# Output projections: first token differences moved to GpSimd, upper tokens stored aside in four pieces

## The chip, the cores and the metric

The kernel runs on one core of one Trainium2 chip, with that core's engines: TensorE for products (PE in the profile; PEld is its weight load), VectorE (DVE), ScalarE (ACT), GpSimd (POOL) and SyncE (SP), which issues most loads. The metric is the device time of one execution in microseconds; lower is better. A comparison rests on the median of several executions.

## The reference

A two-layer encoder step over 512 prompt frames and 128 sample frames (640 tokens in all), with 2048 channels. What matters here is the end of each layer:

```python
y = jnp.concatenate([y_a, y_b, y_c], axis=-1) @ w_out
return x + y, new_conv, new_k, new_v
```

The concatenation has 2048 channels and `w_out` is 2048 x 2048. After the last layer a final RMSNorm is applied. Everything is fp32, and the outputs must hold that precision.

## The kernel before

Activations lie channel-first: `R` holds 16 blocks of 128 channels by 640 tokens. The 640 tokens are cut into two halves of 320: `TA` (lower) and `TB` (upper). A fp32 product is made of three products of split operands: `split` (L136 to L144) writes a high part on ACT (L138, a copy to the reduced type) and a low part on DVE (L139, raw minus high, so both of its inputs lie in SBUF). `HL` holds both parts of the 16 blocks.

Each layer (the loop at L906) runs 36 projections of `w_in` (`proj`, matmuls at L760) with attention, convolution and gates worked in between. When its last gates are done (L1061 multiplies the last of them into `R`), all 16 blocks of `R` are split into `HL` (L1072, L1073), and the output projection begins.

Output columns 0 and 1 are made by `proj` in the plain way. From column 2 on, columns are taken in pairs by `s_pair` (matmuls in `s_mm`, L821), which saves one of eight products of 768 channels by a Strassen-like scheme: sums and differences of weight tiles and of activation blocks. The activation part is made by `combos` (L794), once a layer, and called after column 1 has been written into the program. With `KA` for blocks 10 to 15 and `KB` for blocks 4 to 9, each in two groups of three blocks (10 to 12 and 13 to 15, with 4 to 6 and 7 to 9), it forms for each group, in place in `R`:

- first, R[KA, TA] becomes R[KA, TB] - R[KA, TA] (L804)
- second, R[KA, TB] becomes R[KB, TB] - R[KA, TB] (L805)
- third, R[KB, TB] becomes R[KB, TB] minus the result of the first (L806)
- fourth, inside the loop that splits the results, R[KB, TA] minus the result of the second (L812)

These are eight subtractions a layer of 128 x 960 fp32, all issued through the helper `sub` on DVE (L789). The results are split into `th`, `tl` and, for the one that has its place there, `HL` (L814).

The second subtraction overwrites the upper tokens of blocks 10 to 15. In the last layer those are needed again for the last two output columns, which are made in another way. So they are stored aside in DRAM first (`y12d`, L1074: one DMA of 960 KB issued by GpSimd after the 16 splits) and loaded back near the end (L1098). The second subtraction waits for that store to have read its source.

Instructions stand in the order of each engine's own queue, and an engine works its queue in order. The order is made by a planner from an estimated timeline, with the loads and splits of weights (`s_prep`, `s_split`, `wprep`) at high priority. SP issues the weight loads (L149). GpSimd's queue carries memsets, small copies and many DMAs: the residual of columns 0 and 1 (L1111, into `zt`), the residual of the pairs (L834) and the store aside. Column 0 and 1 are added to their residual on DVE at L1115.

Of the kernel before, what the change touches and what calls it, by code (L numbers as in the profile page):

```python
# [13 lines left out]
ALU = mybir.AluOpType  # L14
# [4 lines left out]
L = 2  # L19
# [39 lines left out]
def build(nc, tc, ctx, A):  # L59
# [15 lines left out]
    def open_pool(n, side):  # L75
        uid[0] += 1
        held_pools[n] = tc.tile_pool(name=f"{n}{uid[0]}", bufs=1, reuse_waits="tile", side=side)
        cur[n] = held_pools[n].__enter__()

    def close_pool(n):  # L80
        held_pools.pop(n).__exit__(None, None, None)

    def tl(shape, tag, bufs, dt=F32, pl=None):
        uid[0] += 1
        pl = pl or (cur[home[tag]] if tag in home else sb)
        return pl.tile(shape, dt, tag=tag, name=f"{tag}_{uid[0]}", bufs=bufs)

    def w25():
        return tl([P, TOK], "w25", 2)
# [22 lines left out]
    ve, ac, gp, pe, sy = nc.vector, nc.scalar, nc.gpsimd, nc.tensor, nc.sync  # L112

    HL = sb.tile([P, 2 * NK, TOK], F32R, tag="HL", name="HL")
    R = sb.tile([P, NK, TOK], F32, tag="R", name="R")
# [8 lines left out]
    ks = Rf[:, (C0 + 3) * TOK + 288:(C0 + 3) * TOK + 288 + P]  # L124
# [4 lines left out]
    y12d = dr.tile([P, 6, HT], F32, tag="y12d", name="y12d")  # L129
# [3 lines left out]
    def half(t):  # L133
        return t.rearrange("p (s n) -> p s n", s=2)

    def split(raw, scale=None, hi=None, lo=None):  # L136
        if scale is None:
            a = ac.activation(hi, raw, AF.Copy)  # L138
            v = ve.tensor_tensor(out=lo, in0=raw, in1=hi.bitcast(F32), op=ALU.subtract)  # L139
        else:  # L140
            a = ac.activation(hi, raw, AF.Copy, scale=scale)
            v = ve.scalar_tensor_tensor(
                out=lo, in0=raw, scalar=scale, in1=hi.bitcast(F32), op0=ALU.mult, op1=ALU.subtract
            )  # L144
        return a.ins, v.ins
# [99 lines left out]
    def lsm(l, base, n=1):  # L245
        o = l * SM_L + base
        return sm[:, o:o + n]
# [149 lines left out]
    for l in range(L):  # L397
        ve.tensor_scalar(
            out=hsm[:, l * 8:(l + 1) * 8], in0=lsm(l, SM_LG, 8), scalar1=0.5, scalar2=None, op0=ALU.mult
# [366 lines left out]
    KS, KB, KA = slice(0, 4), slice(4, 10), slice(10, 16)  # L766
    TA, TB = slice(0, HT), slice(HT, TOK)
# [20 lines left out]
    def sub(out, a, b):  # L788
        ve.tensor_tensor(out=out, in0=a, in1=b, op=ALU.subtract)  # L789

    def hl(ks, cs):
        return HL[:, ks, cs], HL[:, slice(NK + ks.start, NK + ks.stop), cs]

    def combos():  # L794
        T = {}
        tt = [
            (tl([P, 6, HT], f"th{n}", 1, F32R, cur["tt"]), tl([P, 6, HT], f"tl{n}", 1, F32R, cur["tt"]))
            for n in (2, 3, 4)
        ]
        T[2], T[3], T[4] = tt  # L800
        T[1] = hl(KA, TB)
        gs = [(slice(KA.start + g, KA.start + g + 3), slice(KB.start + g, KB.start + g + 3)) for g in (0, 3)]
        for a, b in gs:
            sub(R[:, a, TA], R[:, a, TB], R[:, a, TA])  # L804
            sub(R[:, a, TB], R[:, b, TB], R[:, a, TB])  # L805
            sub(R[:, b, TB], R[:, b, TB], R[:, a, TA])  # L806
        place = {1: (0, TA), 2: (1, TB), 3: (0, TB), 4: (1, TA)}
        for n in (3, 2, 4, 1):
            for g, ab in enumerate(gs):
                i, cs = place[n]  # L810
                if n == 4:
                    sub(R[:, ab[1], TA], R[:, ab[1], TA], R[:, ab[1], TB])  # L812
                ks = slice(3 * g, 3 * g + 3)
                split(R[:, ab[i], cs], None, T[n][0][:, ks, :], T[n][1][:, ks, :])  # L814
        return T
# [90 lines left out]
    for l in range(L):  # L906
# [35 lines left out]
        for n, (kind, i) in enumerate(ZT):  # L942
# [9 lines left out]
            if l == 0 and 2 <= n < 10:  # L952
                for h in (n - 2, n + 6):
                    a = bscr[h:h + 1, :]
# [13 lines left out]
            elif kind == "ag":  # L968
# [5 lines left out]
                    out=half(u[:, HALO:HALO + 512]), in0=t3[:, :, :PT_], scalar=1.0, in1=a3[:, :, :PT_],  # L974
# [3 lines left out]
                    out=us[:, :, HALO:].rearrange("p (s b) n -> p s b n", s=2),  # L978
                    in0=t3[:, :, PT_:].rearrange("p s (b n) -> p s b n", n=ST), scalar=1.0,
                    in1=a3[:, :, PT_:].rearrange("p s (b n) -> p s b n", n=ST), op0=ALU.add, op1=ALU.mult,  # L980
# [7 lines left out]
            elif kind in ("k", "v"):  # L988
# [4 lines left out]
                if kind == "k":  # L993
                    kk = [[tl([P, 512], t + n, 1, F32R) for n in ("h", "l")] for t in ("k", "m")]
                    for h in range(2):
                        for o in range(2):
                            ac.activation(kk[0][h][rows2[o]], raw[rows2[h]], AF.Copy)
                        for o in range(2):
                            ve.tensor_tensor(
                                out=kk[1][h][rows2[o]], in0=raw[rows2[h]], in1=kk[0][h][rows2[h]].bitcast(F32),  # L1000
                                op=ALU.subtract,
                            )
                    gp.dma_start(A["o_kn"][l], ks)
                else:
# [5 lines left out]
                    for h in range(2):  # L1010
# [3 lines left out]
                            out=V[h][:, :, rows2[1 - h]], in0=pt[:, :, rows2[h]], in1=hi.bitcast(F32),  # L1014
                            op=ALU.subtract,
# [7 lines left out]
            elif kind == "q":  # L1023
# [5 lines left out]
                for h in range(2):  # L1029
# [4 lines left out]
                        out=q[rows2[1 - h]], in0=raw[rows2[h]], in1=hi.bitcast(F32), op=ALU.subtract  # L1034
# [33 lines left out]

        close_pool("at")
        open_pool("sw", "left")  # L1070
        for k in range(NK):
            split(R[:, k, :], None, HL[:, k, :], HL[:, NK + k, :])  # L1072
        if l == L - 1:  # L1073
            gp.dma_start(y12d, R[:, KA, TB])  # L1074
        acc = w25()
        resid = A["xT"] if l == 0 else x1d
        done = NK if l == 0 else NK - 2
# [30 lines left out]
        for j in list(range(2)) + list(range(2, done, 2)):  # L1108
            if j < 2:
                res = zt()  # L1110
                gp.dma_start(res, resid[j])  # L1111
                ps = proj(
                    [A["w_out"][l, j][:, c * 512:(c + 1) * 512] for c in range(4)], s_prep if j else wprep
                )
                ve.tensor_tensor(out=half(R[:, j, :]), in0=ps[:, :, :HT], in1=half(res), op=ALU.add)  # L1115
            else:
                s_pair(l, j, T, resid, turn if j + 2 == done else None)
            if j == 0:
                close_pool("wp")
                open_pool("tt", "right")  # L1120
            if j == 1:
                T = combos()
            for i in range(j, j + 1 if j < 2 else j + 2):
                if l == 0:
                    gp.dma_start(x1d[i], R[:, i, :])
                add_sq(i, i == 0, acc)
# [48 lines left out]
    for i, cs in enumerate(parts):  # L1175
        for k in range(NK):
            with tc.issue_after(last["rsqrt"] if k >= 13 else (evac if k >= 10 else added if k >= 2 else evac0).ins):
                ve.scalar_tensor_tensor(  # L1178
                    out=R[:, k, cs], in0=R[:, k, cs], scalar=sm[:, SM_FG + k:SM_FG + k + 1], in1=rows[i],
# [120 lines left out]
```

## Time and profile before

| | us |
|---|---|
| median of 3 runs | 1834.02 (1833.66 to 1834.88) |
| profiled execution, its own time | 1833.57 |
| its span in the trace | 1831.8 |
| PE busy in the span | 1803.6 (98%) |
| DVE busy | 1258.1 (69%) |
| ACT busy | 785.0 (43%) |
| POOL busy | 174.0 (9%) |

Times in rows are microseconds from the start of the span unless marked ns. A row of the timeline gives start, length, engine, line, operation, what is written and read, the count of merged instructions and, in brackets, how long the engine had been idle before and what released it. Two DVE instructions in a row overlap a little in the records: the next one starts before the recorded end of the one ahead, so the pitch from start to start is what an instruction costs its queue.

### The profile page before, as it was taken

What the parts mean: (1) busy time and instruction counts of PE and PEld (TensorE: products, weight loads), DVE (VectorE), ACT (ScalarE), POOL (GpSimd) and SP (SyncE); (2) the same over time, 40 slices, a digit from 0 to 9 for tenths busy, and PEclk for the clock granted to TensorE, in tenths of its full rate; (3) what the DMA queues carried; (4) which work ended last, traced back from release to release, by engine and by line L of the source; (5) the groups of instructions that cost most, each with busy time, mean ns of one, the idle gap of its engine ahead of it and who ended that gap; (6) DMA issues with size and microseconds to landing.
All of it is one profiled execution on the core that took longest, in us unless ns stands there. A gap on an engine that the chain in (4) does not pass through costs nothing.

```text
span 1831.8 us, 32312 instructions
## 1 busy us (share of the span) xinstructions
PE 1803.6 (98%) x12580; PEld 1766.5 (96%) x12580; DVE 1258.1 (69%) x2562; ACT 785.0 (43%) x1593; POOL 174.0 (9%) x383
## 2 busy tenths in 40 slices
PE   8999999999999999999999999999999999999996
PEld 7899999999999999999999999999999999989996
DVE  7959999567555445966686999766655544776765
ACT  7831224556644334533352222555755333533331
POOL 1121210000001010100030010000001110010000
PEclk9999999999999999999999999999999999999998
DMA  8844442222222343533333332222222244442233
GB/s 283 290 129 103 105 130 76 70 64 70 87 78 84 98 162 116 171 134 116 109 102 89 82 81 78 78 67 73 73 84 85 74 139 132 158 160 84 71 113 121
DMA packets 89193, 202.30 MB, mean 110 GB/s; under 512 B 12064, under 2 KB 17104, under 8 KB 89008
## 3 DMA queue, kind: packets, MB, share of 16 engines
q1 hardware_dynamic: 68848, 139.75, 25.3%
q0 software_dynamic: 17728, 57.60, 10.3%
q10 hardware_dynamic: 2464, 2.88, 0.5%
q8 instruction: 99, 1.62, 0.4%
q14 instruction: 54, 0.44, 0.1%
HBM read 184.84 MB, written 20.33 MB: 112 GB/s over the span
## 4 chain that ended last, share of the span: by engine, by line
PE 94%; DVE 3%; DMA 2%; issue 1%; ACT 0%; SPq 0%; DVEq 0%; ACTq 0%; POOLq 0%
PE z L760 59%; PE a L821 9%; PE z L821 9%; PE a L278 2%; PE z L301 2%; PE a L497 2%; PE a L540 2%; PE a L477 2%; PE z L1145 1%; DVE R L1178 1%; PE a L528 1%; DMA wr<-w_in 1%; PE a L647 1%; PE a L673 1%; PE a L686 1%
## 5 line engine op out<-in xcount | busy, mean ns | idle before, releaser
L760 PE MATMUL z<-HL,wh 128*128 128x320 f32 x4992 | 979.5, 312 | 0.0
L760 PEld LDWEIGHTS z<-HL,wh 128*128 128x128 f32 x4992 | 788.9, 188 | 7.9 <-issue 5.3
L760 PE MATMUL z<-HL,wl 128*128 128x320 f32 x2496 | 580.4, 311 | 0.7 <-DVE wl L139 0.7
L760 PEld LDWEIGHTS z<-HL,wl 128*128 128x128 f32 x2496 | 419.3, 188 | 2.0 <-DVE wl L139 1.0
L138 ACT ACTIVATE wh<-wr 128x512 fp32r<-128x512 f32 x316 | 198.7, 629 | 448.6 <-PE z L760 373.1
L139 DVE TENSOR_TENSOR wl<-wr,wh 128x512 fp32r<-128x512 f32 x316 | 218.0, 690 | 172.7 <-ACT wh L138 163.6
L425 DVE SCALAR_TENSOR_TENSOR R<-R,sm 128x128 f32<-128x128 f32 (+1 forms) x480 | 235.4, 552 | 0.1
L138 ACT ACTIVATE sh<-sr 128x768 fp32r<-128x768 f32 (+1 forms) x125 | 98.3, 787 | 206.2 <-PE a L821 91.4
L821 PE MATMUL z<-HL,sh 128*128 128x320 f32 x728 | 160.9, 309 | 1.9 <-ACT sh L138 1.9
L139 DVE TENSOR_TENSOR sl<-sr,sh 128x768 fp32r<-128x768 f32 (+1 forms) x125 | 110.1, 881 | 40.7 <-ACT sh L138 40.5
L821 PEld LDWEIGHTS z<-HL,sh 128*128 128x128 f32 x728 | 121.7, 188 | 2.4 <-ACT sh L138 2.4
L821 PE MATMUL z<-HL,sl 128*128 128x320 f32 x364 | 113.4, 312 | 0.9 <-DVE sl L139 0.7
L139 DVE TENSOR_TENSOR g<-a,g 128x512 fp32r<-128x512 f32 x80 | 49.5, 634 | 39.8 <-ACT g L138 39.2
L821 PE MATMUL a<-th,sh 128*128 128x320 f32 x234 | 72.2, 308 | 0.0
L821 PE MATMUL a<-tl,sh 128*128 128x320 f32 x234 | 72.2, 308 | 0.0
L821 PE MATMUL a<-th,sl 128*128 128x320 f32 x234 | 72.2, 308 | 0.0
L821 PEld LDWEIGHTS z<-HL,sl 128*128 128x128 f32 x364 | 68.3, 188 | 3.2 <-DVE sl L139 3.2
L821 PE MATMUL a<-HL,sh 128*128 128x320 f32 x312 | 68.9, 308 | 0.0
L138 ACT ACTIVATE g<-a 128x512 fp32r<-128x512 f32 x80 | 42.1, 551 | 53.1 <-PE a L531 29.9
L501 DVE CUSTOM_DVE_ANT_0 g<-a,R 128x256 f32<-128x256 f32 (+1 forms) x128 | 46.4, 388 | 23.4 <-PE a L497 20.0
L513 ACT ACTIVATE g<-g,sml 128x256 f32<-128x256 f32 (+1 forms) x128 | 59.8, 468 | 0.0
L485 POOL DMA_DIRECT2D R<-brep x32 | 17.3, 541 | 407.3 <-issue 238.2
(263 smaller groups left out, 2536.0 us busy)
## 6 DMA issues: line engine op xcount, KB each, us to landing
wr<-w_in SPq DMA_DIRECT2D x304, 256.0 KB, 2.7
sr<-w_out SPq DMA_DIRECT2D x52, 384.0 KB, 3.3
sr<-w_out SPq DMA_DIRECT2D x34, 256.0 KB, 2.6
u<-w_mv SPq DMA_DIRECT2D x16, 512.0 KB, 4.0
u<-cmkT POOLq DMA_DIRECT2D x16, 512.0 KB, 3.6
u<-cmv POOLq DMA_DIRECT2D x16, 512.0 KB, 4.3
u<-w_mk SPq DMA_DIRECT2D x14, 512.0 KB, 5.1
R<-xT SPq DMA_DIRECT2D x16, 320.0 KB, 4.7
```

What stands on the lines that cost most here:

```text
L138: a = ac.activation(hi, raw, AF.Copy)
L139: v = ve.tensor_tensor(out=lo, in0=raw, in1=hi.bitcast(F32), op=ALU.subtract)
L278: pe.matmul(ps[ct][:, :256], w[:, ws], mslot(l, k, lo), start=k == 0 and n == 0, stop=k == NK - 1 and n == 2,)
L301: pe.matmul(psv[:, m, :], mslot(l, k, lo)[:, ms], w, start=k == 0 and n == 0, stop=k == NK - 1 and n == 2,)
L425: ve.scalar_tensor_tensor(out=o, in0=x, scalar=w, in1=o, op0=ALU.mult, op1=ALU.add)
L477: pe.matmul(ps[:, :HT], w[:, ws], x[:, k, :], start=n == 0, stop=n == 11)
L497: pe.matmul(ps[:, j, c0:256], q[:, p * P:(p + 1) * P], kk[n][h][:, (p - 1) * P + c0:(p + 1) * P], start=n == 0, stop=n == 1,)
L501: ve.tensor_tensor_reduce(out=x[:, j, c0:], in0=ps[:, j, c0:], in1=bt[:, c0:], scale=1.0, scalar=-3.0e38, op0=ALU.add, op1=ALU.max, accum_ ...
L513: ac.activation(x, x, AF.Exp, bias=ng[:, p:p + 1], accum_out=sm_[:, p:p + 1])
L540: pe.matmul(po[:, os], V[h][:, v, :], p[:, ms], start=v == 0 and n == 0, stop=v == 3 and n == 1, skip_group_check=True,)
L760: pe.matmul(ps[:, s, :HT], w[:, ws], HL[:, lo * NK + k, s * HT:(s + 1) * HT], start=k == 0 and n == 0, stop=k == NK - 1 and n == 2,)
L821: pe.matmul(out, a[:, k * P:(k + 1) * P], b[:, k, :], start=start and k == 0 and i == 0, stop=stop and k == n - 1 and i == 2, skip_group_c ...
```

## The change

In `combos` the first subtraction of both groups is issued on GpSimd in place of DVE, ahead of a loop that holds the second and third of both groups on DVE. The second and third both depend on the first: one overwrites what it reads, the other reads what it writes. It holds for both layers.

In the last layer the store aside is cut into four DMAs, of blocks 10 and 11, 12 and 13, 14, and 15, and stands in the program ahead of the 16 splits in place of behind them. Each piece depends on the final values of its own blocks alone.

```diff
         for a, b in gs:
-            sub(R[:, a, TA], R[:, a, TB], R[:, a, TA])
+            gp.tensor_tensor(out=R[:, a, TA], in0=R[:, a, TB], in1=R[:, a, TA], op=ALU.subtract)
+        for a, b in gs:
             sub(R[:, a, TB], R[:, b, TB], R[:, a, TB])
             sub(R[:, b, TB], R[:, b, TB], R[:, a, TA])
...
         open_pool("sw", "left")
+        if l == L - 1:
+            for g in (0, 2, 4, 5):
+                n = 2 if g < 4 else 1
+                ks = slice(KA.start + g, KA.start + g + n)
+                gp.dma_start(y12d[:, g:g + n, :], R[:, ks, TB])
         for k in range(NK):
             split(R[:, k, :], None, HL[:, k, :], HL[:, NK + k, :])
-        if l == L - 1:
-            gp.dma_start(y12d, R[:, KA, TB])
```

## Rows read from the trace of the kernel before

**Rows 1.** The page's first part: each engine's busy time in the span, share and instruction count.

```profile
PE 1803.6 (98%) x12580; PEld 1766.5 (96%) x12580; DVE 1258.1 (69%) x2562; ACT 785.0 (43%) x1593; POOL 174.0 (9%) x383
```

**Rows 2.** The chain that ended last in order of time (start, length, what), around the start of the second layer's output projection.

```profile
1592.33 4.68 DMA sr<-w_out
1604.64 5.55 DMA y12d<-R
1636.28 9.66 PE z L821 x64
```

**Rows 3.** What TensorE waited for in the second layer's output projections (1600 to 1800 us): engine and line, what it waited for, us in total, times, longest.

```profile
PE z L760 <- DVE sl L139: 2.3, 1, 2.3
PE z L821 <- ACT sh L138: 1.4, 1, 1.4
PE z L821 <- DVE sl L139: 0.7, 2, 0.4
```

**Rows 4.** The same for the first layer's (740 to 980 us).

```profile
PE z L760 <- DVE sl L139: 1.4, 1, 1.4
PE z L821 <- ACT sh L138: 0.5, 1, 0.5
```

**Rows 5.** Timeline of DVE in the second layer, around the combinations. L789 with 128x960 is a subtraction of `combos`.

```profile
1599.78 1.15 DVE L789 TENSOR_TENSOR R<-R 128x960 f32<-128x960 f32 x1
1600.85 0.82 DVE L139 TENSOR_TENSOR HL<-R,HL 128x640 fp32r<-128x640 f32 x1
1603.53 0.82 DVE L1061 TENSOR_TENSOR R<-R,zt 128x640 f32<-128x640 f32 x1
1605.15 0.82 DVE L139 TENSOR_TENSOR HL<-R,HL 128x640 fp32r<-128x640 f32 x1 [0.81 <-ACT HL L138]
1606.01 1.16 DVE L789 TENSOR_TENSOR R<-R 128x960 f32<-128x960 f32 x1
1610.21 3.30 DVE L789 TENSOR_TENSOR R<-R 128x960 f32<-128x960 f32 x3 [3.04 <-DMA y12d<-R]
1614.15 1.15 DVE L789 TENSOR_TENSOR R<-R 128x960 f32<-128x960 f32 x1
...
1620.57 0.69 DVE L139 TENSOR_TENSOR sl<-sr,sh 128x512 fp32r<-128x512 f32 x1
```

**Rows 6.** The same of the first layer, where nothing is stored aside.

```profile
747.85 1.15 DVE L789 TENSOR_TENSOR R<-R 128x960 f32<-128x960 f32 x1
748.92 0.82 DVE L139 TENSOR_TENSOR HL<-R,HL 128x640 fp32r<-128x640 f32 x1
751.60 1.15 DVE L789 TENSOR_TENSOR R<-R 128x960 f32<-128x960 f32 x1
...
753.40 1.15 DVE L789 TENSOR_TENSOR R<-R 128x960 f32<-128x960 f32 x1
754.47 0.82 DVE L139 TENSOR_TENSOR HL<-R,HL 128x640 fp32r<-128x640 f32 x1
755.21 4.61 DVE L789 TENSOR_TENSOR R<-R 128x960 f32<-128x960 f32 x4
...
766.87 0.68 DVE L139 TENSOR_TENSOR sl<-sr,sh 128x512 fp32r<-128x512 f32 x1
```

**Rows 7.** Groups of POOL by form: busy us, mean ns of one, idle time before.

```profile
L563 POOL COPY kc<-R 64x32 f32<-64x32 f32 x16 | 5.1, 318 | 0.6
L570 POOL MEMSET g<- 128x512 f32 x4 | 2.1, 528 | 0.2
L964 POOL MEMSET R<- 128x30 f32 x6 | 0.8, 134 | 5.2 <-ACT zt L254 3.8 <-ACT wh L138 1.4
```

**Rows 8.** Timeline of POOL's small copies from SBUF to SBUF (L563) and of DVE at the same moments, at four places. L139 and L999 have two inputs in SBUF, and so has L425; L586 has one in PSUM and one in SBUF.

```profile
547.67 0.69 DVE L139 TENSOR_TENSOR wl<-wr,wh 128x512 fp32r<-128x512 f32 x1 [1.66 <-ACT wh L138]
547.78 0.64 POOL L563 COPY kc<-R 64x32 f32<-64x32 f32 x1
548.96 0.30 DVE L586 CUSTOM_DVE_ANT_0 g<-a,R 128x144 f32<-128x144 f32 x1
549.01 0.21 POOL L563 COPY kc<-R 64x32 f32<-64x32 f32 x1
...
1400.41 0.69 DVE L139 TENSOR_TENSOR wl<-wr,wh 128x512 fp32r<-128x512 f32 x1 [1.67 <-ACT wh L138]
1400.52 0.65 POOL L563 COPY kc<-R 64x32 f32<-64x32 f32 x1
...
1086.22 0.76 DVE L425 SCALAR_TENSOR_TENSOR R<-R,sm 128x512 f32<-128x512 f32 x1
1086.34 0.70 POOL L563 COPY kc<-R 64x32 f32<-64x32 f32 x1
...
240.18 0.22 POOL L563 COPY kc<-R 64x32 f32<-64x32 f32 x1
240.21 0.75 DVE L999 TENSOR_TENSOR mh<-g,kh 64x512 fp32r<-64x512 f32 x1
...
1088.93 0.69 DVE L999 TENSOR_TENSOR mh<-g,kh 64x512 fp32r<-64x512 f32 x1
```

**Rows 9.** Timeline of POOL from 1583 to 1615 us: its DMA issues around the store aside.

```profile
1603.30 0.54 POOL L1111 DMA_DIRECT2D zt<-x1d  x1 [15.97 <-DVE zt L1060]
1604.64 0.82 POOL L1074 DMA_DIRECT2D y12d<-R  x1 [0.80 <-DVE R L1061]
1605.35 0.65 POOL L1111 DMA_DIRECT2D zt<-x1d  x1
```

**Rows 10.** DMA issues over the whole span: written and read, queue, count, KB each, median us from issue to landing.

```profile
y12d<-R POOLq DMA_DIRECT2D x1, 960.0 KB, 5.5
x1d<-R POOLq DMA_DIRECT2D x16, 320.0 KB, 2.9
o_kn<-R POOLq DMA_DIRECT2D x2, 64.0 KB, 2.8
o_cp<-R POOLq DMA_DIRECT2D x8, 15.0 KB, 1.8
y<-y12d POOLq DMA_DIRECT2D x1, 960.0 KB, 7.8
```

## The prediction

> **What bounds the kernel now.** I read the busy shares first: TensorE is busy 98% of the span and the vector engine 69%, GpSimd 9% [rows 1]. So a change that touches only DVE and POOL can win nothing but time in which TensorE waits. The chain that ended last, in order of time, says where that is: the matmuls follow one another, except at the start of the second layer's output projection, where the chain passes through two transfers, the second of them the store aside, 1604.64 to 1610.19, and comes back to TensorE at 1636.28 [rows 2]. The reader is to see there that this store is the one thing of the change that the chain holds.
>
> The view of TensorE's own waits then prices it. In the second layer's output projections it waited 2.3 + 1.4 + 0.7 = 4.4 us [rows 3], in the first layer's 1.4 + 0.5 = 1.9 us [rows 4]. That is the whole stake: 6.3 us, 0.34% of 1834. All these waits end on DVE or on an ACT split, and the DVE rows show what stands ahead. In the second layer the piece of weights that TensorE wants is split at 1620.57, behind the subtractions, and there is a hole of 3.04 us at 1610.21 in which DVE waits for the store [rows 5]. In the first layer there is no store and no hole, the split at 766.87 is still late, by a DVE queue that is full [rows 6]. So from 1599 (and 747) on, an extra microsecond in DVE's queue is an extra microsecond of TensorE, and one saved is one gained until 4.4 (or 1.9) us are used up.
>
> **The change, part by part.** The profiled execution took 1833.57 us (span 1831.8 and 1.8 around it), 0.45 below the median of 1834.02. The sum is made on the former and 0.45 is added at the end.
>
> *Removed from DVE:* two subtractions a layer. Start to start one costs its queue 1600.85 - 1599.78 = 1.07 us, in the first layer 748.92 - 747.85 = 1.07 [rows 5, 6]. 2.14 us a layer.
>
> *Added to POOL:* two subtractions of 960 columns, two inputs in SBUF each. No such operation is in the trace. The nearest rows are POOL's memsets: 512 columns in 528 ns, 30 in 134 ns [rows 7], so 0.82 ns a column and about 0.1 us to start; one pass over 960 columns would be 0.9 us. That is the lower end. Two reads in turn with the write beside them are two passes, 1.7 us; two reads and a write in turn are three, 2.5 us. I take 2.1, between two and three passes: the one POOL operation with an SBUF input in the trace, a copy of 32 columns, takes 0.21 us undisturbed [rows 8], more than the memset of 30, so an input isn't free.
>
> By the Trainium skill (GPSIMD Engine Reference, Performance versus the Vector engine) a fp32 tensor_tensor of 2048 columns takes 4497 ns on GpSimd; scaled to 960 that is an estimate of 2.1 us, and no run here shows it yet.
>
> *Does DVE work on meanwhile?* This decides the sign of the gp part. The rows say no. POOL's copies that start while a DVE instruction with two SBUF inputs runs take 0.64, 0.65 and 0.70 us in place of 0.21, and end about 0.06 us after that DVE instruction does (547.78 + 0.64 = 548.42 against 547.67 + 0.69 = 548.36; the others alike). A copy beside L586, with one input in PSUM, is not stretched (0.21) [rows 8]. Something is held by one of the two for a whole instruction. The other direction is barely visible since the copies are so short: one that got in at 240.18 goes with a DVE instruction of 0.75 us where its like takes 0.69 [rows 8]. It also got in while DVE instructions followed back to back, so POOL isn't starved. Nearly all DVE work around `combos` has two SBUF inputs (the splits, the gates, the subtractions). So I let each gp subtraction take its 2.1 us out of DVE's time.
>
> The Trainium skill speaks against this change here: SBUF — State Buffer, Who interferes with whom, says that a DVE instruction with two SBUF inputs contends with a GpSimd instruction that reads SBUF, and that whoever comes second blocks fully. By that rule the sum below stands; without it the first rival's does. The trace agrees in the direction that it shows (0.64 to 0.70 against 0.21 us).
>
> *First layer.* Each of the two subtractions takes 2.1 in place of 1.07 us: 2 x 1.03 = 2.06. The second group has no cover: its gp subtraction can start only when the last split has read its block (755.2), and the second and third subtractions behind it wait for it, with the splits of the results behind them; I put 0.3 for the signals both ways. Sum +2.4 us, on a queue for which TensorE waits already.
>
> *Second layer.* The pieces of blocks 10 to 13 are final and landed before they are needed, so the second and third subtraction of the first group move ahead of the wait, as they stand in the first layer (751.60, 753.40) [rows 6]. The queue up to the last gate (L1061 ended 1604.3) grows by 1.03 (first gp subtraction) and 1.07 (second subtraction of group one, now ahead): 1606.4. The third fits into the 0.81 us for which DVE waits for ACT there. The last split then ends at 1608.0 in place of 1605.9, the second gp subtraction at 1610.1, with a signal 1610.3. The last piece isn't later: issued 0.3 us after 1606.4, as the whole was after its gate (1604.64 against 1604.35) [rows 5, 9], and landed 1.8 to 2.9 us on, as writes of 15 to 320 KB do [rows 10], at 1608.5 to 1609.6. Before, DVE had four of the second and third subtractions to do from 1610.2 on; now two from 1610.3 on: -2.14 + 0.1, about -2.0 us. It is under 4.4, so TensorE gets it.
>
> *At nothing:* three more DMA issues on POOL, 0.5 to 0.8 us each [rows 9], on an engine with 9% busy; behind them is the residual of column 0, issued at 1603.30 for an addition that comes at 1613.42 or later, and that cover is some 5 us. The load of the aside copy (7.8 us) [rows 10] comes only behind the pairs.
>
> **Sum:** +2.4 - 2.0 = +0.4 us: 1833.57 + 0.4 + 0.45 = 1834.4. With 1.7 us a subtraction it is 4 x 0.4 = 1.6 lower, 1832.8; with 2.5 it is 1836.0; with 0.9 the last piece decides the second layer and the sum is near 1830. The likeliest case's own range is 1832 to 1836.5, with the planner's order free to move a microsecond.
>
> **Rivals.** *The two engines do overlap, or the gp time falls into DVE's holes.* Then the first layer loses 2.14 from DVE's queue and gives back some 1.2 in the wait of the second group: -0.9. In the second the last gate stays where it is (-1.07 + 1.07), the second gp subtraction ends at 1608.1, two subtractions are left in place of four: -2.1 - 2.1 = -4.2, nearly all of its 4.4. Together -5.1: 1829. For it: the 3.04 us hole, DVE instructions with one SBUF input (an evacuation, an addition) that the planner may place there; against it the stretched copies. 0.23.
>
> *Slower: POOL's order.* POOL works its queue in order, and now holds four pieces, two loads of residuals and two subtractions. If the planner sets the last piece behind the second gp subtraction, it goes out at 1610.3, lands 2.9 us on with its issue, and the second subtraction starts at 1613.5 in place of 1610.3: +3.2. If it sets the first gp subtraction behind the pieces of blocks 14 and 15, that one waits for the last gate, and both run one after the other past 1606: some +3 too. With the +0.4 that is 1837.8. It decides as soon as one piece and one subtraction change places. For it: the order is made from estimates that may price POOL wrongly; against it: block 15 is final 1.6 us before its last split has been read, so an order by readiness puts the piece first. 0.19.
>
> *The cut does nothing:* the last piece lands as late as the whole did. Even then the gp subtraction of the second group ends at 1610.3 and hides it; the time is the forecast's.
>
> **How the numbers follow.** Forecast 0.58 (the last case included), overlap 0.23, POOL's order 0.19. About 0.2% (3.7 us) is what a measurement of this kernel can tell from no change: 1830.4 and 1837.7 bound "same". Overlap is mostly below (0.19 of its 0.23), POOL's order mostly above (0.15), the forecast within but for 0.03 at the upper and 0.02 at the lower end: faster 0.21, same 0.61, slower 0.18. The range takes in the better part of both rivals: 1829.5 to 1838.
>
> **What would show it.** In the changed profile: POOL rows of 128x960 of 1.7 to 2.5 us, longer if they wait for the port; DVE instructions with two SBUF inputs beside them stretched or set apart by about that; the wait for the store on DVE gone, a wait for POOL of some 2 us in its place; TensorE's waits near 4.3 us in the first layer and 2.4 in the second. DVE rows of ordinary length beside a running gp subtraction would make the first rival right; a last piece issued after it, the second. The prediction is wrong at its root if the two waits of TensorE don't follow DVE's queue one for one.

## The result, and the profile after

The changed kernel took 1838.54 us (median of 8) where the kernel before took 1834.50 in the runs beside it: ratio 1.0026, 95% interval 1.0017 to 1.0034. It is slower by some 4 us, outside the predicted range of 1829.5 to 1838.0, and on the side to which 0.18 had been given. The profiled execution took 1838.78, its span 1837.0.

What TensorE waited for, first layer (730 to 1000 us) and second (1590 to 1810), answering to [rows 3, 4]:

```profile
PE z L760 <- DVE sl L139: 3.4, 1, 3.4
PE z L822 <- ACT sh L138: 0.5, 1, 0.5
PE z L822 <- DVE sl L139: 0.3, 2, 0.2
...
PE z L760 <- DVE sl L139: 3.4, 1, 3.4
PE z L760 <- ACT sh L138: 0.4, 1, 0.4
PE z L822 <- DVE sl L139: 0.2, 1, 0.2
```

In the first layer the waits grew from 1.9 to 4.2 us, in the second they went from 4.4 to 4.0, but gathered mostly into one wait. That sums to +1.9, and the span grew by 5.2. The page's first part says where the rest is:

```profile
PE 1808.4 (98%) x12580; PEld 1771.7 (96%) x12580; DVE 1256.9 (68%) x2558; ACT 785.1 (43%) x1593; POOL 187.7 (10%) x390
```

For the same 12580 matmuls TensorE was busy 4.8 us longer than in the kernel before (1803.6 [rows 1]), and idle only 0.4 us longer over the whole span. So most of the loss isn't waiting, it is matmuls that took longer, and that is for the most part the clock. The windows of 4 us around the two waits (start and end, length, busy us of PE, PEld, DVE, ACT, POOL, then the granted clock, the DMA share and GB/s):

```profile
764.00:768.00 4.00, 1.75 (x11) 1.23 (x9) 4.00 (x5) 1.48 (x3) 1.24 (x3) 1.00 0.00 0
768.00:772.00 4.00, 2.74 (x10) 2.74 (x11) 3.97 (x6) 0.00 (x0) 1.94 (x4) 0.62 0.98 346
772.00:776.00 4.00, 4.00 (x28) 4.00 (x27) 1.59 (x3) 1.85 (x2) 0.00 (x0) 0.95 0.37 150
776.00:780.00 4.00, 4.00 (x29) 4.00 (x28) 3.62 (x4) 2.37 (x3) 2.13 (x4) 1.00 0.54 172
...
1620.00:1624.00 4.00, 3.00 (x19) 2.48 (x17) 4.00 (x5) 3.01 (x5) 0.00 (x0) 1.00 0.27 82
1624.00:1628.00 4.00, 1.21 (x4) 1.21 (x5) 4.00 (x5) 0.00 (x0) 3.17 (x6) 0.72 0.61 191
1628.00:1632.00 4.00, 4.00 (x16) 4.00 (x16) 2.03 (x3) 0.01 (x1) 0.02 (x1) 0.50 0.80 301
1632.00:1636.00 4.00, 4.00 (x27) 4.00 (x27) 2.12 (x2) 1.99 (x3) 0.00 (x0) 0.93 0.20 69
1636.00:1640.00 4.00, 4.00 (x29) 4.00 (x28) 3.85 (x5) 2.33 (x4) 2.67 (x5) 1.00 0.65 200
```

Read the clock column downward in each group: 1.00 ahead of the wait, down to 0.62 and 0.50 at its end and behind it (0.50 is 1.2 GHz for the whole window, 1.00 is 2.4 GHz), and 1.00 again from 776 and 1636 on. In the kernel before, the same windows stand at 1.00 throughout. The chain shows what that costs: the 44 matmuls behind the wait.

```profile
754.89 3.12 POOL R L804
762.19 2.35 DVE tl L139 x3
766.38 2.22 DVE tl L139 x2
769.26 8.15 PE z L760 x44
...
1612.43 3.11 POOL R L804
1619.72 2.35 DVE tl L139 x3
1623.91 2.22 DVE tl L139 x2
1626.79 9.32 PE z L760 x44
```

In the kernel before the 44 of the first layer took 6.73 us. Those of the second, of which these are the first and the last row, took 6.72 (1621.31 to 1628.03), behind a wait of 2.3 us:

```profile
1621.31 0.56 PE L760 MATMUL z<-HL,sl 128*128 128x320 f32 x2 [2.33 <-DVE sl L139]
...
1627.57 0.46 PE L760 MATMUL z<-HL,sl 128*128 128x320 f32 x2
```

So the half clock cost 1.4 and 2.6 us in this execution, 4.0 of the 4.8 us by which TensorE was busy longer. The sum of waits and clock, 5.9, is above the 5.2 of the span; the first layer's output projection began 0.8 us earlier than in the kernel before (735.48 and 734.71 in the two chains), and what else evens it out isn't placed. The chain also names what stands ahead of the wait: a GpSimd subtraction, and then result splits (`tl`) on DVE, in place of the store aside, which is gone from the chain.

DVE and POOL in the first layer show how they share the time:

```profile
745.01 0.69 DVE L139 TENSOR_TENSOR sl<-sr,sh 128x512 fp32r<-128x512 f32 x1
745.03 2.81 POOL L804 TENSOR_TENSOR R<-R 128x960 f32<-128x960 f32 x1 [11.18 <-DVE HL L139]
745.62 0.82 DVE L734 SCALAR_TENSOR_TENSOR zt<-z,rstd 128x640 f32<-128x640 f32 x1
746.35 2.90 DVE L139 TENSOR_TENSOR HL<-R,HL 128x640 fp32r<-128x640 f32 x2
...
754.73 1.15 DVE L789 TENSOR_TENSOR R<-R 128x960 f32<-128x960 f32 x1
754.89 3.11 POOL L804 TENSOR_TENSOR R<-R 128x960 f32<-128x960 f32 x1 [1.05 <-DVE HL L139]
758.03 2.35 DVE L789 TENSOR_TENSOR R<-R 128x960 f32<-128x960 f32 x2 [2.16 <-POOL R L804]
761.04 1.15 DVE L789 TENSOR_TENSOR R<-R 128x960 f32<-128x960 f32 x1
762.11 6.49 DVE L139 TENSOR_TENSOR tl<-R,th 128x960 fp32r<-128x960 f32 x6
768.52 1.29 DVE L139 TENSOR_TENSOR sl<-sr,sh 128x512 fp32r<-128x512 f32 x2
```

The first GpSimd subtraction is recorded from 745.03, but the DVE split with two SBUF inputs runs to 745.70; 2.81 us long, the subtraction ends at 747.84, 2.1 us after it got in. Then L734 (one input in PSUM) runs beside it at its ordinary 0.82. The two splits with two SBUF inputs that follow take 2.90 together, where such a pair takes 1.56 elsewhere in this trace: the first of them sits until 747.84. The second subtraction waits for a DVE subtraction to end at 755.88 and takes 2.1 us more; DVE has nothing beside it and stands for 2.16 us. And the weight splits (`sl` at 768.52) now come behind all six result splits; in the kernel before the first of them stood behind five in the first layer, and behind three in the second.

### The profile page after: what moved, and what is told of

Same layout as the page of the kernel before. It is cut to its first block, busy times and chain, and to the rows that moved or that the text cites. A ratio compares the mean times of both kernels' runs of the same rounds, so it can differ in the third digit from the quotient of the medians.

```text
span 1837.0 us, 32318 instructions
## 1 busy us (share of the span) xinstructions
PE 1808.4 (98%) x12580; PEld 1771.7 (96%) x12580; DVE 1256.9 (68%) x2558; ACT 785.1 (43%) x1593; POOL 187.7 (10%) x390
## 4 chain that ended last, share of the span: by engine, by line
PE 94%; DVE 3%; DMA 1%; issue 1%; POOL 0%; ACT 0%; SPq 0%; DVEq 0%; POOLq 0%; ACTq 0%
PE z L760 59%; PE a L822 9%; PE z L822 8%; PE a L278 3%; PE z L301 2%; PE a L497 2%; PE a L540 2%; PE a L477 2%; PE z L1149 1%; DMA sr<-w_out 1%; DVE R L1182 1%; PE a L528 1%; PE a L647 1%; PE a L673 1%; PE a L686 1%
## 5 line engine op out<-in xcount | busy, mean ns | idle before, releaser
L139 DVE TENSOR_TENSOR wl<-wr,wh 128x512 fp32r<-128x512 f32 x316 | 217.6, 689 | 171.8 <-ACT wh L138 162.7
L425 DVE SCALAR_TENSOR_TENSOR R<-R,sm 128x128 f32<-128x128 f32 (+1 forms) x480 | 235.1, 550 | 0.1
L139 DVE TENSOR_TENSOR sl<-sr,sh 128x768 fp32r<-128x768 f32 (+1 forms) x125 | 110.5, 885 | 47.2 <-ACT sh L138 47.0
L139 DVE TENSOR_TENSOR g<-a,g 128x512 fp32r<-128x512 f32 x80 | 49.5, 634 | 39.9 <-ACT g L138 39.3
```

The costliest lines, as they stand in the source:

```text
L425: ve.scalar_tensor_tensor(out=o, in0=x, scalar=w, in1=o, op0=ALU.mult, op1=ALU.add)
```

## The experiments

Two theories were held against each other. Theory: the GpSimd subtractions shut DVE out, which lengthens its queue; the order of the weight splits makes it worse; and a TensorE wait that gets long enough halves the clock behind it. Rival: the pieces of the store aside do it, by their transfers or by POOL's order. Times are medians; in brackets the difference to the kernel before in the runs beside it and the ratio's interval.

**e1, the four pieces alone.** The first subtraction back on DVE.

```diff
-            gp.tensor_tensor(out=R[:, a, TA], in0=R[:, a, TB], in1=R[:, a, TA], op=ALU.subtract)
-        for a, b in gs:
+            sub(R[:, a, TA], R[:, a, TB], R[:, a, TA])
```

> The four-piece store alone; all eight subtractions on DVE in the old program order. Theory (the GpSimd subtractions take the port and lengthen DVE's queue, the planner then sets the weight splits behind all six result splits, and a TensorE wait of 3.4 us brings its clock down): without them the first layer is as in the kernel before (waits 1.9 us, clock 1.00), and the second loses the 3.04 us hole: waits of TensorE 4.4 become about 2, so 1831.5 to 1833 where the kernel before has 1834.5. Rival (the pieces' transfers meet the weight loads, DVE waits for the weights): the second layer stays as late as in the changed kernel, TensorE waits 3.5 us or more there, clock down, 1836 to 1837.

1830.29 (-4.0; 0.9975 to 0.9992). The pieces are a gain, larger than the 1.5 to 3 us expected, and the rival as the main cause falls. It is not wholly wrong: the second layer's TensorE wait was 2.4 us, and DVE waited for the second weight piece:

```profile
1599.94 0.69 DVE L139 TENSOR_TENSOR sl<-sr,sh 128x512 fp32r<-128x512 f32 x1 [1.47 <-ACT sh L138]
```

**e2, the GpSimd subtractions alone.** The store aside is put back to one DMA behind the splits, as in the kernel before; `combos` is the changed one.

> The GpSimd subtractions alone; the store aside is one DMA behind the splits, as before. Theory: the first layer as in the changed kernel (TensorE waits 3.4 us at once, clock down to about 0.83 in ten us, +4 us), the second about as before, since the hole of the store covers the GpSimd time: 1837.5 to 1839. Rival (the pieces are the cause): the loss shrinks to the first layer's queue alone, +2 us or less, 1836.5 at most, clock 1.00 in the second layer.

1840.49 (+6.2; 1.0022 to 1.0048), dearer than expected: TensorE waited 3.4 us at once in the first layer and 4.6 in the second, with the half clock behind both (the 44 matmuls took 9.41 and 8.27 us). The loss is all in this part. That the hole of the store would cover the GpSimd time was wrong: the first subtraction stands ahead of the last gate and so holds up the store, and DVE's hole grew from 3.04 to 4.17 us.

**e3, the changed kernel with the order of the weight splits set.** From the fourth result on the low-part split is queued behind the third weight piece's split, from the fifth on behind the fourth's.

```diff
-        split(raw, None, hi, lo)
+        sls.append(split(raw, None, hi, lo)[1])
...
-                split(R[:, ab[i], cs], None, T[n][0][:, ks, :], T[n][1][:, ks, :])
+                done_ += 1
+                with tc.issue_after(sls[-1] if done_ > 4 else sls[-2]) if done_ > 3 else nullcontext():
+                    split(R[:, ab[i], cs], None, T[n][0][:, ks, :], T[n][1][:, ks, :])
```

> The changed kernel with one thing more: in combos the low-part splits of results 4 and on stand behind the weight split of the third piece of column 1, from the fifth on behind that of the fourth, so that the weight splits stand where they stood before the change or earlier. Theory (order and clock cost more than the port): TensorE's waits fall from 3.4 to under 2 us in each layer, the clock stays at 1.00, and 4 to 5 us come back: 1833 to 1834.5. Rival (the port's lock alone lengthens the queue, the order makes no difference): waits stay over 3 us, 1837 to 1838.5.

1835.50 (+1.2; 0.9999 to 1.0017), between the two expectations. Of the changed kernel's 4 us some 3 came back. The wait for the weight split fell to 0.2 us in each layer, but waits of up to 1.4 us appeared for splits on ACT and DVE further on, and in its profile the clock still dipped behind them: two groups of 64 matmuls took 11.2 us, where the kernel before has 9.66 for such a group [rows 2].

```profile
780.97 11.20 PE z L827 x64
...
1638.37 11.19 PE z L827 x64
```

**e4, the four pieces with the same set order.** The edits of e1 and e3 together.

> The four-piece store with all subtractions on DVE, and the same order of weight splits as in the kernel with the changed order. Theory: TensorE hardly waits (under 1 us in each layer), 1829 to 1831, faster than both kernels. Rival (the wait moves to the products of the results that now are split later): 1832.5 or more, with TensorE waiting for the result splits (tl) or for sums of weights at L821 in place of the weight split.

1832.20 (-2.1; 0.9980 to 0.9998). Not below e1, and nearer to the rival's 1832.5 than to the 1831 of the theory. In its profile TensorE waited no more for the weight split, but 1.6 + 0.4 and 1.7 + 0.4 us for splits at the pair products; the clock stayed at 1.00. Without the GpSimd part this order wins nothing over the planner's: the waits sum to 4.1 us here and to 4.5 in e1, so it moved them and took hardly any away.

**e5, memset in the subtraction's place.** The same place in POOL's queue and the same order on DVE, but POOL only writes; the kernel leaves out the first subtraction.

```diff
-            gp.tensor_tensor(out=R[:, a, TA], in0=R[:, a, TB], in1=R[:, a, TA], op=ALU.subtract)
+            gp.memset(R[:, a, TA], 0.0)
```

> The changed kernel with a GpSimd memset to zero in place of each first subtraction, which leaves out that part of the computation. POOL then writes SBUF but reads nothing, 0.9 us a group by the memset rows, and the result splits stand in the same order as in the changed kernel, all six ahead of the weight splits. Theory (a GpSimd instruction that reads SBUF shuts out DVE instructions with two SBUF inputs): no DVE instruction is stretched beside the memsets, DVE has two subtractions less, TensorE waits about 0.5 us for the weight split in each layer, clock 1.00: 1827.5 to 1829.5. Rival 1 (any GpSimd instruction does it, or the order alone): the splits beside the memset are stretched, or TensorE still waits over 2 us: 1833 or more.

1831.60 (-2.9; 0.9974 to 0.9992), above the 1829.5 expected, yet 7 us below the changed kernel with the same six result splits ahead of the weight splits. DVE beside the memsets:

```profile
745.21 0.91 POOL L804 MEMSET R<- 128x960 f32 x1 [10.46 <-DVE HL L139]
745.64 0.69 DVE L139 TENSOR_TENSOR sl<-sr,sh 128x512 fp32r<-128x512 f32 x1 [0.49 <-ACT sh L138]
...
755.18 1.16 DVE L789 TENSOR_TENSOR R<-R 128x960 f32<-128x960 f32 x1
755.21 0.90 POOL L804 MEMSET R<- 128x960 f32 x1 [1.03 <-DVE HL L139]
```

Neither stretches the other: two SBUF inputs on DVE (0.69, 1.16) run beside a POOL instruction that only writes, and POOL starts while they run. So what shuts DVE out is a POOL instruction that reads, not any POOL instruction. What the order costs alone e5 doesn't say: DVE has two subtractions less than in e1, 2.14 us a layer, and the memset is also shorter than the subtraction for which the second group waits. In its profiled execution (1833.32, 1.7 above the median) TensorE still waited 2.0 us in the second layer, with the half clock behind it; that this lifts the median above the expectation is not shown.

**e6, only the first group on GpSimd.**

```diff
-            gp.tensor_tensor(out=R[:, a, TA], in0=R[:, a, TB], in1=R[:, a, TA], op=ALU.subtract)
+            if a.start == KA.start:
+                gp.tensor_tensor(out=R[:, a, TA], in0=R[:, a, TB], in1=R[:, a, TA], op=ALU.subtract)
+            else:
+                sub(R[:, a, TA], R[:, a, TB], R[:, a, TA])
```

> The changed kernel with only the first group's subtraction on GpSimd, the second group's (the one for which DVE waits with nothing beside it) back on DVE. Theory: one lock of about 1.2 us net and the same order of the weight splits remain, the hole of 2.16 us goes: TensorE waits 2.3 to 3 us in each layer, 1833 to 1836. Rival (the hole of the second group is the whole loss): as the four pieces alone, 1830 to 1831.

1837.10 (+2.6; 1.0005 to 1.0023), dearer than either side expected: all but 1.4 us of the change's loss is there with one subtraction a layer. Waits of 2.3 and 3.4 us, half clock behind both. The hole of 2.16 us is a minor part. Nor is it mainly the length of the first subtraction: in the first layer it held DVE up by 1.34 us (a pair of splits at 2.90 for 1.56) where 1.07 was saved, and the sixth result split, which stands ahead of the weight split here too, adds 1.07. The queue grew more by the planner's order than by GpSimd.

**e7 and e8, DVE's queue made longer without GpSimd.** On e1, one or two further subtractions of 128x960 a layer on DVE, into a tile that is overwritten later (`gs[:2]` in e8).

```diff
+        for a, b in gs[:1]:
+            sub(T[4][1][:, a.start - KA.start:a.stop - KA.start, :], R[:, a, TB], R[:, b, TB])
```

> The four pieces alone, all subtractions on DVE, and one more DVE subtraction of 128x960 in each layer, whose result is overwritten: DVE's queue is 1.07 us longer, no GpSimd arithmetic. Theory (TensorE follows DVE's queue one for one): TensorE's wait for the weight split grows from 1.4 to 2.4 us in the first layer; clock mostly 1.00: +2 to +3 us over the four pieces alone, 1832.5 to 1833.5. Rival (the length of DVE's queue is not what counts): unchanged, 1830.5.

> As the run with one, with two more subtractions in each layer: DVE's queue is 2.14 us longer. Theory: TensorE's wait for the weight split grows to 3.5 us in the first layer and the clock falls behind it, as in the changed kernel: +4.3 us of waits and 2 to 4 us of clock, 1836.5 to 1838.5. Rival (the clock falls because of something in the GpSimd part): waits 3.5 us with the clock at 1.00, 1834.5 to 1835.

e7 1835.25 (+0.8; 0.9993 to 1.0011), dearer than expected, e8 1838.18 (+3.7; 1.0012 to 1.0030), as expected. Two more DVE instructions a layer, 4.3 us in all, take the four pieces from -4.0 (or -2.4, e11) to +3.7: they cost 6 to 8 us and give the changed kernel's time with no GpSimd arithmetic. DVE's queue in these two places is worth 1.4 to 1.8 times its length. e8's profiled execution, the shortest of its ten (1834.32), waited 3.2 us in each layer; in the first layer the clock stayed at 1.00 behind it.

**e9, e10 and e11, the pieces' transfers.** e9: e1 with blocks 10 and 11 stored before they are final, so that the last two output columns work on other values; the piece went out at 1368.80 where e11 issues it at 1592.97, thus 224 us early and not some 100. e10: e1 with those two blocks apart, five pieces, which computes everything. e11: e1 again, beside them. The edit of e10 against e1:

```diff
-            for g in (0, 2, 4, 5):
-                n = 2 if g < 4 else 1
+            for g in (2, 0, 4, 1, 5):
+                n = 2 if g == 2 else 1
```

> The four pieces alone, but blocks 10 and 11 are stored aside some 100 us too early, when they don't hold their final values; the input of the last two output columns is thus not the right one, and nothing else changes. Theory (the piece of blocks 10 and 11, 320 KB at 1593 us, meets the loads of the weight pieces of column 1, which land 6.5 us after issue in place of about 5): the second weight piece's split is no longer waited for (1.47 us on DVE), the last gate comes 1.5 us earlier, TensorE waits 1 us less in the second layer: 1828.5 to 1829.5, about 1.3 below the four pieces run beside it. Rival (the weights are late for another reason): no difference.

> The four pieces alone, with blocks 10 and 11 apart, so five pieces in the order in which blocks become final; it computes everything. Theory of the meeting transfers: only 160 KB go out at 1593 us, about half of the 1.5 us comes back: 1829.3 to 1830, about 0.6 below the four pieces run beside it. Rival: no difference.

> The four pieces alone, once more, beside the runs with five pieces and with the early piece: 1830 to 1831 where the kernel before has 1834 to 1834.5.

e9 1829.82 (-4.1; 0.9962 to 0.9982), e10 1830.07 (-3.8; 0.9972 to 0.9990), e11 1831.52 (-2.4; 0.9979 to 0.9997). The transfers do meet. DMA issues of e11 from 1588 to 1612 us (written and read, queue, count, KB, median us to landing):

```profile
sr<-w_out SPq DMA_DIRECT2D x4, 256.0 KB, 6.5
y12d<-R POOLq DMA_DIRECT2D x1, 320.0 KB, 6.1
```

The same of e10, with the two blocks apart:

```profile
sr<-w_out SPq DMA_DIRECT2D x4, 256.0 KB, 5.5
y12d<-R POOLq DMA_DIRECT2D x2, 160.0 KB, 3.3
```

And of e9, which has no store aside there but the last block's:

```profile
sr<-w_out SPq DMA_DIRECT2D x4, 256.0 KB, 5.1
```

In e10 and e9 the weight pieces land 1.0 to 1.4 us earlier than in e11, and TensorE's wait in the second layer was 2.4 us in e11, 1.3 in e10 and 1.4 in e9. They came out 1.7 and 1.5 us below e11, each more than expected (1.3 and 0.6). The five pieces beat the kernel before; by how much they beat the four lies within the spread between e1 and e11.

## Why the prediction was wrong

*That DVE pays the GpSimd time in full: right for the second group, too much for the first.* 2.1 us was taken for one subtraction; it took 2.1 from the moment at which it got in, and 2.26 for the least disturbed of the four. The second group's kept DVE standing for 2.16 and 2.15 us. The first group's held it up by 1.34 us in the first layer, where L734 ran beside it, and by 0.54 in the second, where most of it fell into a hole in which DVE waited for a weight piece (this split takes 0.69 undisturbed):

```profile
1601.79 2.26 POOL L804 TENSOR_TENSOR R<-R 128x960 f32<-128x960 f32 x1 [4.71 <-DVE HL L139]
1603.37 1.23 DVE L139 TENSOR_TENSOR sl<-sr,sh 128x512 fp32r<-128x512 f32 x1 [1.67 <-ACT sh L138]
```

The rule of the Trainium skill (SBUF — State Buffer, Who interferes with whom), by which a DVE instruction with two SBUF inputs and a GpSimd instruction that reads SBUF contend, holds here in both directions: pairs of splits at 2.90 for 1.56 us, POOL at 2.81 to 3.11 for 2.26, and no stretching beside memsets (e5) or with one input in PSUM (L734). The rival by which the two engines overlap is out, though its other half, that the GpSimd time falls into DVE's holes, held in this one place.

*First layer, +2.4 us: the sum came out by luck.* The third weight split came at 768.52 for 766.87 [rows 6] in a stage that began 0.77 us earlier (the last matmuls ahead of it in the chain start at 734.71, before at 735.48): 2.4 us later. But the subtractions, which were to give all of it, give 1.36 (1.34 - 1.07 and 2.16 - 1.07); the other 1.07 is the sixth result split that the planner moved ahead, and that was in no term. TensorE's longest wait rose by 2.05, somewhat less than the queue, and the layer's waits are 4.2 us where 4.3 was named.

*The step that failed is the price of a TensorE wait.* It was taken at its length. Behind a long one the granted clock halves, and that was in no term: 1.4 us in the first layer and 2.6 in the second of the profiled execution. It isn't this execution alone: the mean granted clock is on record for each, and lies at 0.993 to 0.995 in all eight of the changed kernel, while 23 of the 27 of the kernel before that ran beside e1 have 0.996. A difference of 0.002 of 1837 us is 3.7 us, an estimate, and a rough one as these values are rounded to 0.001. "The prediction is wrong at its root if the two waits of TensorE don't follow DVE's queue one for one" named the right place, but had the wait itself in mind and not what stands behind it. e8 shows it without GpSimd: 4.3 us of DVE cost 6 to 8.

*Second layer, -2.0 us: wrong as well.* The waits fell by 0.4, to 4.0 us where 2.4 was named. Two terms were missing. First the planner's order, allowed "a microsecond": six result splits ahead of the weight split in place of three, 3 x 1.07 = 3.2 us, which is more than the 2.0 forecast as won. e3 gives 3 us back over both layers by the order alone. Second the pieces under "at nothing": their queue entries are free, their transfers aren't. The weight pieces landed later, the last gate came at 1609.73, 2.45 us later than before once the 3.75 us are taken off by which the layer's end was late (1586.34 for 1582.59 in the chains); 2.1 was forecast, from the subtractions alone, and that this is near is luck too: 1.91 of the 2.45 is the second weight piece, whose split came that much later by the same measure (1603.37 for 1597.71), and 0.54 is what the first subtraction held up; the subtraction that left DVE and the one that moved ahead cancel. In e1, with no GpSimd arithmetic, that split came as late (1599.94, in a layer that began 0.37 us later). e9 and e10 price the transfers at 1.0 to 1.1 us of wait. The hole of the store did go, as forecast, and e1 and e11 show the pieces as 4.0 and 2.4 us won.

*POOL's order: out.* The last piece went out ahead of the second subtraction:

```profile
1610.84 0.55 POOL L1076 DMA_DIRECT2D y12d<-R  x1 [1.86 <-DVE R L1062]
1611.38 0.54 POOL L1115 DMA_DIRECT2D zt<-x1d  x1
1612.43 3.10 POOL L804 TENSOR_TENSOR R<-R 128x960 f32<-128x960 f32 x1 [0.52 <-DVE HL L139]
```

1837.8 (its own terms, 1834.4 + 3.2, give 1837.6) was near the measured time by another mechanism.

How the loss splits between the lock, the order and the clock isn't additive, since each lengthens the same wait: a memset in the subtraction's place takes 7 us off the changed kernel (e5), the order 3 (e3), the second group 1.4 (e6). What can be added up is DVE's queue against e1: 1.36 us in the first layer and 0.55 in the second (0.54 - 1.07 and 2.15 - 1.07) from the subtractions, and 1.07 in each from the sixth result split. So the planner's order lengthened it as much as the subtractions did, 2.1 and 1.9 us.

## What to carry to other kernels

Moving work from a full engine to an idle one is a gain only if the two don't shut each other out: here a subtraction on GpSimd held up by as much as 2.16 us a vector engine that needed 1.07 for the same work. It also changes the order that a planner sets elsewhere, so compare the queues of both kernels. Where a slow stretch stands behind a long wait, as here, price the wait by its length and by that stretch (1.3 to 2.7 us), and look whether a change gathers several short waits into one long one. In a change of two parts, run each alone: the four pieces won 2 to 4 us, and the subtractions lost 6.

## What the runs showed of the hardware that wasn't expected

The half clock is not certain. Longest wait of TensorE in each layer where one wait for the weight split stood ahead of the 44 matmuls, with how long these took:

| wait, us | 44 matmuls, us |
|---|---|
| 1.0, 1.0, 1.0, 1.3, 1.4, 1.4, 1.4, 1.6 (e5, e10, e11, e10, before, e1, e9, e9) | 6.72 to 6.73 in each |
| 2.0 (e5), 2.3 (e6), 2.4 (e1) | 8.27, 8.27, 8.26 |
| 2.3 (before) | 6.72 |
| 2.4 (e11) | 6.73 |
| 2.6 (e7) | 8.02 |
| 3.2, 3.2 (e8) | 6.73, 8.24 |
| 3.3 (e7) | 6.72 |
| 3.4 (changed, both layers), 3.4 (e6), 3.4 (e2), 4.6 (e2) | 8.15, 9.32, 8.26, 9.41, 8.27 |

None of these eight waits of up to 1.6 us was followed by the half clock, and ten of the fourteen of 2.0 us and more were. e1 and e11 are one kernel with the same wait and fell on different sides, 8.26 against 6.73. One long wait isn't the only way to it: in e3 waits of 1.4 and 0.4 us, with a few matmuls between them, were followed by it in both layers, while the kernel before has the same pair in its second layer [rows 3] and stayed at 1.00. So executions of one kernel can differ by 1.3 to 2.7 us for each such place, and a profile shows one draw of it. The runs of e8 spread from 1834.32 us, at a mean granted clock of 0.996, to 1842.41, at 0.993; two such places explain 5.4 us of these 8.1 at most, and the rest is open.
